# First weights and first memory features in four interleaved pieces, five identity products ahead, x behind the first chunk's weights

## The chip, the core and the metric

The kernel runs on one NeuronCore of a Trainium2 chip. TensorE (PE) multiplies, VectorE (DVE) and ScalarE (ACT) do elementwise work, GpSimd (POOL) does a few masks and powers, and SyncE (SP) issues every transfer (DMA) between HBM and the core's memory. The engines run on their own and wait for each other by semaphores; on each of them instructions run in the order in which they were built. The metric is device microseconds of one execution, the median of three runs. Lower is better.

## The reference, cut to what matters

One layer over 256 tokens of x and 256 tokens of a memory, model width 2048, all in float32:

```python
h = rms_norm(x, norm_mix_g)
x = x + hybrid_mixer(h, ...)              # h @ w_in (18464 columns), two recurrent branches, @ w_out
mem_n = rms_norm(mem, norm_mem_g)
k, v = split(mem_n @ w_kv, 2)             # w_kv: 2048 x 4096
x = x + cross_attention(rms_norm(x, norm_x_g), k, v) @ w_xo
x = x + square(relu(rms_norm(x, norm_ffn_g) @ w_ff1)) @ w_ff2
out = rms_norm(x, norm_final_g)
```

The part at stake is the very beginning: `v`, the right half of `mem_n @ w_kv`, is what the kernel computes first, together with turning x into features.

## The kernel before, in words

**Products in three parts.** Each float32 weight tile `raw` is split into a rounded half `whi` (ACT, L108) and a rest `wlo` (DVE, L111); each activation in the same way into the two halves of a tile `q`. A product is then three matmuls: `q` high by `whi` (L151), `q` high by `wlo` (L152), `q` low by `whi` (L153), each 128x512, summed in PSUM.

**Chunks and quarters.** `chunk` makes 512 output columns from 2048 contracted features, in four quarters `q` of 512 features. `fetch` loads one quarter of weights (1 MB, `raw`, three buffers) and splits it in two halves, so a quarter has two `whi` and two `wlo` tiles and 24 matmuls (4 features blocks by 2 token tiles by 3). The first two chunks are `values(0)` and `values(1)`, then `values(2)` and `values(3)` and the `blocks` of `w_in` follow; below they are chunk 0, chunk 1 and so on. Between chunks 2 and 3 stands the first `blocks` call (L193, L194), which needs the features of x.

**Memory's features.** In chunk 0, `load_mem(c)` loads 512 features of `mem` (`xc`, 0.5 MB), transposes them on PE with the identity (8 transposes, L242), and ACT and DVE make the two halves of `q` (L255, L256) with the norm's gain, which `load_gains` has loaded (`grow`) and transposed (L228). For the first quarter, mem and weights are each loaded in two pieces (`pieces`, `rush`), and the features' transposes are held until after the first rounding (`issue_after(rushed[0])`).

**x's features.** `load_rows(c, x, 0)` loads x in four pieces (0.5 MB each); ACT squares and sums them (L271); their rows' scale goes over PE to `rrow` (L283, L284); PE transposes x (L344, 32 transposes), ACT copies each pair of blocks to `xt` (L347, two buffers), a DMA stores it to `xt_d` (L348), DVE and ACT make `xn` and the features `q` of x (L351, L354, L355). A third `xt` has to wait until the store of the first has landed.

**What sets the order.** The tile framework orders instructions by priorities (`high_priority`) and by when it believes operands are ready; the built order on each engine is then fixed. Every DMA goes over SP's queue, and each takes the next of eight completion counters in turn: a transfer is not issued before the eighth transfer ahead of it has landed. `issue_after` pins an instruction behind another one in SP's or PE's order.

**Small work in the same stretch.** Convolution rows (`cw_rows`), `positions`, `inv_freq`, `gdn_norm_g`, `a_log`, `dt_bias` are loaded early for later use; ACT makes eight decay masks `dm_w` (L514, stored to `dm_d`), sines and cosines (L413, L416), each change of function costing an ACT_TABLE_LOAD.

## Time and profile before

| | us |
|---|---|
| median of three runs | 2099.76 |
| lowest and highest run | 2099.24, 2100.12 |
| profiled execution | 2099.76 |
| its span, from the first to the last instruction | 2098.0 |
| PE busy in it | 2081.5 |
| DVE busy | 1407.9 |
| ACT busy | 1090.9 |

The profiled execution is the median of the runs, so a difference worked out from its trace is also one against the median; 1.76 us of its time lie outside the span. A row of the timeline says when a group of equal instructions began, how long it lasted, engine, line, operation, and in brackets how long the engine had stood idle before it and what ended that. Overlapping matmuls are pipelined, so the distance of starts, not the duration, is the price of one.

### The profile page before, as it was taken

What the parts mean: (1) busy time and instruction counts of PE and PEld (TensorE: products, weight loads), DVE (VectorE), ACT (ScalarE), POOL (GpSimd) and SP (SyncE); (2) the same over time, 40 slices, a digit from 0 to 9 for tenths busy, and PEclk for the clock granted to TensorE, in tenths of its full rate; (3) what the DMA queues carried; (4) which work ended last, traced back from release to release, by engine and by line L of the source; (5) the groups of instructions that cost most, each with busy time, mean ns of one, the idle gap of its engine ahead of it and who ended that gap; (6) DMA issues with size and microseconds to landing.
All of it is one profiled execution on the core that took longest, in us unless ns stands there. A gap on an engine that the chain in (4) does not pass through costs nothing.

```text
span 2098.0 us, 28725 instructions
## 1 busy us (share of the span) xinstructions
PE 2081.5 (99%) x11172; PEld 1797.4 (86%) x11172; DVE 1407.9 (67%) x2217; ACT 1090.9 (52%) x1700; POOL 28.7 (1%) x39
## 2 busy tenths in 40 slices
PE   8999999999999999999999999999999999999998
PEld 6888888888888888888888899888888888888887
DVE  5766788778758885878557666766556555645655
ACT  7674664565446444655456555554434434444444
POOL 0000000000000000000000000000000000000000
PEclk9999999999999999999999999999999999999999
DMA  8787655556555655555458665566566556656653
GB/s 297 242 272 250 198 188 189 164 172 194 180 162 183 193 179 157 188 186 189 160 177 257 193 187 156 177 199 194 188 200 185 198 189 192 192 190 199 185 198 141
DMA packets 314169, 405.91 MB, mean 193 GB/s; under 512 B 16288, under 2 KB 222128, under 8 KB 313904
## 3 DMA queue, kind: packets, MB, share of 16 engines
q1 hardware_dynamic: 313744, 403.55, 60.7%
q8 instruction: 87, 1.43, 0.3%
q10 hardware_dynamic: 288, 0.52, 0.1%
q14 instruction: 50, 0.41, 0.1%
HBM read 390.40 MB, written 13.65 MB: 193 GB/s over the span
## 4 chain that ended last, share of the span: by engine, by line
PE 95%; DMA 2%; ACT 1%; SPq 1%; DVE 1%; issue 0%; POOLq 0%; POOL 0%; ACTq 0%
PE s L193 33%; PE s L194 17%; PE s L152 13%; PE s L153 13%; PE s L151 13%; PE b L689 2%; DMA xt_d<-xt 1%; DMA xc<-x 1%; PE b L595 1%; ACT whi L108 1%; PE b L121 0%; PE b L123 0%; PE b L122 0%; SPq L292 0%; DVE wlo L111 0%
## 5 line engine op out<-in xcount | busy, mean ns | idle before, releaser
L111 DVE TENSOR_TENSOR wlo<-raw,whi 128x1024 fp32r<-128x1024 f32 x702 | 858.1, 1223 | 525.4 <-ACT whi L108 519.0
L108 ACT ACTIVATE whi<-raw 128x1024 fp32r<-128x1024 f32 x702 | 742.8, 1059 | 739.2 <-PE s L153 388.0
L193 PE MATMUL s<-q,whi 128*128 128x512 f32 x3088 | 1062.8, 390 | 0.3 <-DVE q L959 0.3
L194 PE MATMUL s<-q,wlo 128*128 128x256 f32 x3088 | 845.2, 281 | 0.8 <-DVE wlo L111 0.8
L193 PEld LDWEIGHTS s<-q,whi 128*128 128x128 f32 x3088 | 570.9, 188 | 110.0 <-DVE q L959 0.5
L194 PEld LDWEIGHTS s<-q,wlo 128*128 128x128 f32 x3088 | 579.3, 188 | 14.0 <-DVE wlo L111 2.4
L152 PE MATMUL s<-wlo,q 128*128 128x512 f32 x1264 | 495.3, 392 | 1.4 <-DVE wlo L111 1.3
L153 PE MATMUL s<-whi,q 128*128 128x512 f32 x1264 | 493.0, 390 | 0.0
L151 PE MATMUL s<-whi,q 128*128 128x512 f32 x1264 | 453.3, 391 | 1.5 <-ACT q L255 1.5
L152 PEld LDWEIGHTS s<-wlo,q 128*128 128x128 f32 x1264 | 237.6, 188 | 50.9 <-DVE wlo L111 3.4
L151 PEld LDWEIGHTS s<-whi,q 128*128 128x128 f32 x1264 | 237.2, 188 | 50.6 <-ACT q L255 1.9
L153 PEld LDWEIGHTS s<-whi,q 128*128 128x128 f32 x1264 | 237.7, 188 | 48.1
L200 ACT ACTIVATE bo<-s 128x256 f32<-128x256 f32 x193 | 73.1, 379 | 120.3 <-PE s L194 107.3
L201 DVE TENSOR_TENSOR bo<-bo,s 128x256 f32<-128x256 f32 x193 | 80.3, 416 | 46.4 <-ACT bo L200 46.1
L548 DVE SCALAR_TENSOR_TENSOR acc<-bo,cw,acc 128x255 f32<-128x255 f32 (+2 forms) x144 | 66.8, 479 | 1.5
L650 DVE TENSOR_TENSOR pr<-lw,tw 32x31 f32<-32x31 f32 (+15 forms) x124 | 40.4, 326 | 8.8 <-DMA lw<-scr_l 6.9
L652 DVE TENSOR_TENSOR tw<-tw,pr 32x31 f32<-32x31 f32 (+15 forms) x124 | 40.6, 327 | 2.1
L796 ACT ACTIVATE gth<-s 128x512 f32<-128x512 f32 x32 | 18.9, 592 | 23.8 <-PE s L153 18.3
L998 DVE SCALAR_TENSOR_TENSOR res<-s,rstd3q,res 128x512 f32<-128x512 f32 (+1 forms) x32 | 22.3, 735 | 11.7 <-PE s L153 11.7
L987 DVE SCALAR_TENSOR_TENSOR hs<-bo 128x256 f32<-128x256 f32 x64 | 26.9, 421 | 1.1
L990 DVE TENSOR_TENSOR q<-hs,q 128x256 fp32r<-128x256 f32 x64 | 26.9, 420 | 0.8 <-ACT q L989 0.8
L545 ACT ACTIVATE acc<-bo,cw 128x256 f32<-128x256 f32 x48 | 24.1, 503 | 4.5 <-DVE bo L201 4.4
(292 smaller groups left out, 1083.6 us busy)
## 6 DMA issues: line engine op xcount, KB each, us to landing
raw<-w_in SPq DMA_DIRECT2D x144, 1024.0 KB, 5.2
raw<-w_ff SPq DMA_DIRECT2D x128, 1024.0 KB, 5.4
raw<-w_xkv SPq DMA_DIRECT2D x31, 1024.0 KB, 9.2
raw<-w_out SPq DMA_DIRECT2D x16, 1024.0 KB, 6.1
raw<-w_xq SPq DMA_DIRECT2D x16, 1024.0 KB, 6.6
raw<-w_xo SPq DMA_DIRECT2D x16, 1024.0 KB, 5.2
dec_d<-dec_w SPq DMA_DIRECT2D x8, 384.0 KB, 4.6
dec<-dec_d SPq DMA_DIRECT2D x8, 384.0 KB, 3.2
```

The source lines that it names most:

```text
L108: rounding = act.activation(hi, src, AF.Copy)
L111: vec.tensor_sub(lo, src, hi.bitcast(F32))
L151: pe.matmul(o, xh, wh, start=first, stop=False)
L152: pe.matmul(o, xh, wl, start=False, stop=False)
L153: pe.matmul(o, xl, wh, start=False, stop=last)
L193: pe.matmul(ps[b], lh, xhl, start=kk == 0, stop=False)
L194: pe.matmul(ps[b][:, :S], ll, xh, start=False, stop=kk == KT - 1)
L200: act.activation(o, ps[b][:, S:], AF.Copy)
L201: vec.tensor_add(o, o, ps[b][:, :S])
L548: vec.scalar_tensor_tensor(acc[:, d:], ps[:, :S - d], cw[:, j, blk:blk + 1], acc[:, d:], op0=ALU.mult, op1=ALU.add)
L652: vec.tensor_sub(tw[:, j + 1:32, 0:j + 1], tw[:, j + 1:32, 0:j + 1], pv)
L689: pe.matmul(pv[:, i, :], lhs(i), rhs[:, i, :], start=True, stop=True)
```

## The change

Five parts. (1) The first quarter of chunk 0 is loaded in four pieces of 128 features, each a piece of mem (0.125 MB) followed by a piece of weights (0.25 MB); `rush_mem` is called around each weight load. The weights are split piece by piece (128x512 instead of 128x1024), and each piece of features is transposed (2 transposes) and made into `q` on its own. (2) The gains are loaded behind the first pair of pieces instead of ahead of everything. (3) Five products of the identity with itself run ahead on PE. (4) The loads of x may not be issued before the last weights of chunk 0 are. (5) A later chunk (the last `sig_gate` chunk of the mixer) that shared the switch `rush` loads its first weights in one transfer again instead of two; its call of `take_back(0)`, which does nothing, is left out.

```diff
-    rushed = []
-
-    steps = []
+    fetched, steps = [], []
...
-    def fetch(pieces, k, n, rush=False, hold=None, at=(0, 0)):
+    def fetch(pieces, k, n, rush=None, hold=None, at=(0, 0)):
...
-                for ks in ((slice(0, k // 2), slice(k // 2, k)) if rush else (slice(0, k),)):
-                    nc.sync.dma_start(rv[:, ks, off:off + ap.shape[1]], src[:, ks, :])
+                for ks in ([slice(i, i + 1) for i in range(k)] if rush else [slice(0, k)]):
+                    if rush:
+                        rush(0, ks.start)
+                    fetched.append(nc.sync.dma_start(rv[:, ks, off:off + ap.shape[1]], src[:, ks, :]).ins)
+                    if rush:
+                        rush(1, ks.start)
...
-                rounding = act.activation(hi, src, AF.Copy)
-                if rush and not i:
-                    rushed.append(rounding.ins)
-                vec.tensor_sub(lo, src, hi.bitcast(F32))
+                for ks in ([slice(j * n, (j + 1) * n) for j in range(k // 2)] if rush else [slice(None)]):
+                    act.activation(hi[:, ks], src[:, ks], AF.Copy)
+                    vec.tensor_sub(lo[:, ks], src[:, ks], hi[:, ks].bitcast(F32))
...
     with tc.high_priority(offset=200000):
-        load_gains(0, (norm_mem_g,))
+        heat = bank()
+        for i in range(5):
+            pe.matmul(heat[:, :P], ident, ident, start=True, stop=True)
...
     def load_mem(c):
-        with tc.high_priority(offset=50000):
-            xc = load_rows(c, mem, 50000 if c else 100000, 1 if c else 2)
-            with tc.high_priority(offset=100000), nullcontext() if c else tc.issue_after(rushed[0]):
-                ins = to_feature(lambda t, f: xc[:, t, f * P:(f + 1) * P], G_MEM + 4 * c, memq[c])
+        xc = new_rows()
+        with tc.high_priority(offset=100000):
+            load_rows(c, mem, xc)
+        with tc.high_priority(offset=150000):
+            ins = to_feature(lambda t, f: xc[:, t, f * P:(f + 1) * P], G_MEM + 4 * c, memq[c])
         mem_rows.append((xc, ins))
+
+    def rush_mem(now, f):
+
+        if not f and not now:
+            mem_rows.append((new_rows(), None))
+        xc = mem_rows[0][0]
+        if not now:
+            load_rows(0, mem, xc, slice(f * P, (f + 1) * P))
+            return
+        if not f:
+            load_gains(0, (norm_mem_g,))
+        ps = bank()
+        for t in range(NT):
+            pe.transpose(ps[:, t * P:(t + 1) * P], xc[:, t, f * P:(f + 1) * P], ident)
+        qh, ql = (a[:, f, :] for a in memq[0])
+        g = gains[:, G_MEM + f:G_MEM + f + 1]
+        ins = act.activation(qh, ps[:, :S], AF.Copy, scale=g).ins
+        vec.scalar_tensor_tensor(ql, ps[:, :S], g, qh.bitcast(F32), op0=ALU.mult, op1=ALU.subtract)
+        mem_rows[0] = (xc, ins)
...
     values(0)
+    first_weights = list(fetched)
...
-    xcs = [load_rows(c, x, 0) for c in range(4)]
+    xcs = [new_rows() for _ in range(4)]
+    with tc.issue_after(first_weights[-1]):
+        for c in range(4):
+            load_rows(c, x, xcs[c])
```

On PE at the program's start, before (`xc_117` and `xc_162` are the first and second 512 features of mem, `whi_109` and `wlo_110` the first half of the first weights):

```order
L228 MATMUL b_86<-ident_75,grow_84 128x16
L242 MATMUL b_120<-ident_75,xc_117 128x128
L242 MATMUL b_129<-ident_75,xc_117 128x128
L242 MATMUL b_120<-ident_75,xc_117 128x128 x3
L242 MATMUL b_129<-ident_75,xc_117 128x128 x3
L151 MATMUL s0_104<-whi_109,q_98 128x512
L151 MATMUL s1_105<-whi_109,q_98 128x512
L152 MATMUL s0_104<-wlo_110,q_98 128x512
L152 MATMUL s1_105<-wlo_110,q_98 128x512
L153 MATMUL s0_104<-whi_109,q_98 128x512
L153 MATMUL s1_105<-whi_109,q_98 128x512
L242 MATMUL b_164<-ident_75,xc_162 128x128 x4
```

The same place in the changed program (`xc_108` is the first mem tile, `whi_142` and `wlo_143` the first weights; lines have moved by two):

```order
L234 MATMUL b_84<-ident_75 128x128 x5
L228 MATMUL b_113<-ident_75,grow_111 128x16
L326 MATMUL b_116<-ident_75,xc_108 128x128 x2
L326 MATMUL b_123<-ident_75,xc_108 128x128 x2
L326 MATMUL b_130<-ident_75,xc_108 128x128 x2
L153 MATMUL s0_105<-whi_142,q_99 128x512
L154 MATMUL s0_105<-wlo_143,q_99 128x512
L153 MATMUL s1_106<-whi_142,q_99 128x512
L154 MATMUL s1_106<-wlo_143,q_99 128x512
L326 MATMUL b_137<-ident_75,xc_108 128x128 x2
L155 MATMUL s0_105<-whi_142,q_99 128x512
L155 MATMUL s1_106<-whi_142,q_99 128x512
```

The first products stand behind three pieces of mem instead of all four pieces' worth; further down, not shown, the 8 transposes of the third 512 features moved from inside the second quarter to just ahead of it.

On SP, between the loads of x and the first weights of chunk 1 (`raw_502`), before, with the completion counter that each transfer waits for (`raw_290` holds the last weights of chunk 0):

```order
L362 DMA cw_rows_641<-conv_w 48x128 [waits DMAHW0_49]
L362 DMA cw_rows_641<-conv_w 48x128 [waits DMAHW1_49]
L383 DMA posi_667<-positions 128x256 [waits DMAHW2_49]
L98 DMA raw_290<-w_xkv 128x4x512 [waits DMAHW3_49,DVE_49]
L387 DMA invf_669<-inv_freq 64x1 [waits DMAHW4_49]
L387 DMA invf_669<-inv_freq 64x1 [waits DMAHW5_49]
L428 DMA gdng_705<-gdn_norm_g 128x128 [waits DMAHW6_49]
L433 DMA alog_707<-gdn_a_log 16x1 [waits DMAHW7_49]
L434 DMA dtb_708<-gdn_dt_bias 16x1 [waits DMAHW0_49]
L515 DMA dm_d_718<-dm_w_1261 128x256 [waits DMAHW1_49]
L515 DMA dm_d_718<-dm_w_1376 128x256 [waits DMAHW2_49]
L98 DMA raw_502<-w_xkv 128x4x512 [waits DMAHW3_49,DVE_49]
```

The same in the changed program (`xc_377` to `xc_379` are the second to fourth pieces of x, `raw_518` the first weights of chunk 1; the last weights of chunk 0 stand two rows above):

```order
L294 DMA xc_377<-x 128x2x512 [waits DMAHW2_49]
L294 DMA xc_378<-x 128x2x512 [waits DMAHW3_49]
L294 DMA xc_379<-x 128x2x512 [waits DMAHW4_49]
L387 DMA cw_rows_657<-conv_w 48x128 [waits DMAHW5_49]
L387 DMA cw_rows_657<-conv_w 48x128 [waits DMAHW6_49]
L408 DMA posi_683<-positions 128x256 [waits DMAHW7_49]
L412 DMA invf_685<-inv_freq 64x1 [waits DMAHW0_49]
L412 DMA invf_685<-inv_freq 64x1 [waits DMAHW1_49]
L453 DMA gdng_721<-gdn_norm_g 128x128 [waits DMAHW2_49]
L458 DMA alog_723<-gdn_a_log 16x1 [waits DMAHW3_49]
L459 DMA dtb_724<-gdn_dt_bias 16x1 [waits DMAHW4_49]
L99 DMA raw_518<-w_xkv 128x4x512 [waits DMAHW5_49,DVE_49]
```

Chunk 0's last weights now stand ahead of x; chunk 1's first weights stand behind all of x and behind the small loads, two of which (`alog`, `dtb`) wait for the counters of the third and fourth piece of x.

On ACT, around the last copies `xt` of x's blocks, before (`whi_826`, `whi_830` are the last quarter's weights of chunk 2):

```order
L347 ACTIVATE xt_465<-b_460 128x512
L347 ACTIVATE xt_478<-b_473 128x512
L108 ACTIVATE whi_792<-raw_790 128x1024
L354 ACTIVATE q_357<-xn_466 128x2x256
L354 ACTIVATE q_358<-xn_479 128x2x256
L108 ACTIVATE whi_796<-raw_790 128x1024
L347 ACTIVATE xt_491<-b_486 128x512
L108 ACTIVATE whi_826<-raw_824 128x1024
L354 ACTIVATE q_358<-xn_492 128x2x256
L108 ACTIVATE whi_830<-raw_824 128x1024
```

The same in the changed program (`whi_842` and `whi_846` are the last quarter's weights of chunk 2):

```order
L372 ACTIVATE xt_481<-b_476 128x512
L379 ACTIVATE q_373<-xn_469 128x2x256
L372 ACTIVATE xt_494<-b_489 128x512
L112 ACTIVATE whi_842<-raw_840 128x1024
L379 ACTIVATE q_373<-xn_482 128x2x256
L372 ACTIVATE xt_507<-b_502 128x512
L379 ACTIVATE q_374<-xn_495 128x2x256
L112 ACTIVATE whi_846<-raw_840 128x1024
```

The last copy stood ahead of the first half of that quarter's weights and now stands between the two halves. PE's order is the same in both programs from the first `blocks` call on.

## Rows read from the trace of the kernel before

**Rows 1.** The page: span, PE's busy time, and the group of all weight rests
```profile
span 2098.0 us, 28725 instructions
...
PE 2081.5 (99%) x11172; PEld 1797.4 (86%) x11172; DVE 1407.9 (67%) x2217; ACT 1090.9 (52%) x1700; POOL 28.7 (1%) x39
...
L111 DVE TENSOR_TENSOR wlo<-raw,whi 128x1024 fp32r<-128x1024 f32 x702 | 858.1, 1223 | 525.4 <-ACT whi L108 519.0
```

**Rows 2.** Windows (stretch, length, busy by engine, PEclk, DMA share, GB/s)
```profile
86.72:2085.00 1998.28, 1997.25 (x10770) 1728.73 (x10769) 1346.23 (x2097) 1023.35 (x1582) 24.66 (x26) 1.00 0.60 190
...
16.00:18.00 2.00, 2.00 (x10) 1.63 (x9) 2.00 (x4) 1.95 (x6) 0.00 (x0) 1.00 1.05 388
...
75.00:76.00 1.00, 0.73 (x4) 0.42 (x3) 1.00 (x2) 1.00 (x2) 0.00 (x0) 1.00 1.02 289
```

**Rows 3.** Span and mean granted clock of the core
```profile
core 0: 2098.0 us, clock 0.999
```

**Rows 4.** PE's timeline (start, us, engine, line, operation, idle before and releaser)
```profile
5.89 1.54 PE L242 MATMUL b<-ident,xc 128*128 128x128 f32 x6 [0.74 <-DMA xc<-mem]
8.95 1.22 PE L151 MATMUL s<-whi,q 128*128 128x512 f32 x2 [1.52 <-ACT q L255]
9.97 1.10 PE L152 MATMUL s<-wlo,q 128*128 128x512 f32 x2
10.87 1.05 PE L153 MATMUL s<-whi,q 128*128 128x512 f32 x2
...
13.28 0.56 PE L151 MATMUL s<-whi,q 128*128 128x512 f32 x1
...
17.58 0.62 PE L151 MATMUL s<-whi,q 128*128 128x512 f32 x2
18.03 1.03 PE L242 MATMUL b<-ident,xc 128*128 128x128 f32 x8
...
31.44 0.50 PE L152 MATMUL s<-wlo,q 128*128 128x512 f32 x1 [0.57 <-DVE wlo L111]
...
36.56 0.62 PE L151 MATMUL s<-whi,q 128*128 128x512 f32 x2
37.02 0.40 PE L152 MATMUL s<-wlo,q 128*128 128x512 f32 x1
...
51.77 0.50 PE L152 MATMUL s<-wlo,q 128*128 128x512 f32 x1 [0.50 <-DVE wlo L111]
...
75.75 0.50 PE L152 MATMUL s<-wlo,q 128*128 128x512 f32 x1 [0.27 <-DVE wlo L111]
...
81.57 0.50 PE L152 MATMUL s<-wlo,q 128*128 128x512 f32 x1
...
86.72 0.39 PE L193 MATMUL s<-q,whi 128*128 128x512 f32 x1
```

**Rows 5.** ACT's timeline: roundings that waited for a transfer, one table load
```profile
7.48 1.06 ACT L108 ACTIVATE whi<-raw 128x1024 fp32r<-128x1024 f32 x1 [4.12 <-DMA raw<-w_xkv]
...
13.52 1.06 ACT L108 ACTIVATE whi<-raw 128x1024 fp32r<-128x1024 f32 x1 [0.24 <-DMA raw<-w_xkv]
...
34.52 2.01 ACT L108 ACTIVATE whi<-raw 128x1024 fp32r<-128x1024 f32 x2 [3.51 <-DMA raw<-w_xkv]
...
47.08 1.28 ACT L514 ACT_TABLE_LOAD   x1
```

**Rows 6.** SP's timeline: the first issue, and the first weights of chunk 1
```profile
0.79 0.40 SPq L226 DMA_DIRECT2D grow<-norm_mem_g  x1
...
28.84 1.00 SPq L98 DMA_DIRECT2D raw<-w_xkv  x2
```

**Rows 7.** The tile xt (min/median/max ns, first and last start in us)
```profile
L347 ACT ACTIVATE xt<-b x8: 587/598/601, 58.3 to 78.7; 128x512 f32<-128x512 f32 x8
```

**Rows 8.** The chain of waits: stores of xt that ended last
```profile
58.92 4.25 DMA xt_d<-xt
...
72.31 6.32 DMA xt_d<-xt
```

More of the change, by code (lines that the diff above doesn't have):

```diff
@@ L1 @@
 import math
[L2 removed]
+from contextlib import ExitStack
 import numpy as np
@@ L135, in quad_a, with chunk @@
         return new_quad(hqp, 5)
-    def chunk(quads, pieces_of, evac, before=None, hold=None):
+    def chunk(quads, pieces_of, evac, before=None, rush=None, hold=None):
         ps = stream_ps()
@@ L158, in chunk @@
                     before(q)
-                halves = fetch(pieces_of(q), 4, 512, rush=before is not None and q == 0)
-                if before and not q:
-                    before(q)
+                halves = fetch(pieces_of(q), 4, 512, rush=None if q else rush)
                 for i in range(4):
@@ L285, in scale_row, with new_rows, load_rows @@
         return row
-    def load_rows(c, src, rush, pieces=1):
-        xc = kv.tile([P, NT, 512], F32, name="xc", tag="xc", bufs=8)
+    def new_rows():
+        return kv.tile([P, NT, 512], F32, name="xc", tag="xc", bufs=8)
+    def load_rows(c, src, xc, fs=slice(0, 512)):
         rows = src[0, :, c * 512:(c + 1) * 512].rearrange("(t p) d -> p t d", p=P)
-        with tc.high_priority(offset=rush):
-            for ts in (slice(i * NT // pieces, (i + 1) * NT // pieces) for i in range(pieces)):
-                nc.sync.dma_start(xc[:, ts, :], rows[:, ts, :])
-        return xc
+        nc.sync.dma_start(xc[:, :, fs], rows[:, :, fs])
     def row_squares(xc, ssq, c):
```

3 lines of the change are left out of this document (1 added, 2 removed).

## The prediction

> **What bounds the kernel now.** I read the page first: PE is busy for 2081.5 of 2098.0 us [rows 1]. The windows tell where the rest can be: from the first `blocks` call at 86.72 us to 2085 us PE is busy for 1997.25 of 1998.28 us, 1.03 us idle in all [rows 2], and PE's order there is the same in both programs. So the change can only shift the moment at which that stretch begins, and everything behind follows by the same amount. I therefore read PE's timeline up to 86.72 [rows 4] and look for time that isn't matmul work at full pace.
>
> There are three kinds. First, PE's products begin at 8.95, after waiting for `q`, which waited for mem and for the rounding of weights that landed at 7.48 [rows 4, 5]. Second, they begin slowly: two products that wait for nothing start 0.45 us each (9.97 to 10.87), while two later ones take 0.23 each (36.56 to 37.02) [rows 4]. The granted clock of the core is 0.999 over the span [rows 3], which leaves about 2 us of full-rate time, or 4 us at half rate; the pace places them between 8.95 and 13.28: that is 1.2 GHz against 2.4. PEclk in the windows reads 1.00 [rows 2] and is too coarse to show it. Third, three stalls of 0.57, 0.50 and 0.27 us on `wlo` [rows 4].
>
> **The change part by part.** I follow PE through both orders and note how far the changed program is ahead at fixed places.
>
> *First products.* Before, 1,032 KB (8 of gains, 512 of mem, 512 of weights) were on the core at 7.48 [rows 5]. Now the first product needs two weight pieces and three mem pieces, 904 KB: 128 KB less, 0.34 us at 388 GB/s [rows 2], and the bulk starts first, 0.40 us of issue for the gains earlier [rows 6]. That is about 6.75; then the two transposes of the third piece at the slow pace and the copy to `q` behind the second rounding, 0.7 to 0.9 us. First product at about 7.5, 1.4 us earlier; bounds 7.0 and 8.9 (below).
>
> *Small pieces.* A row of mem is now 512 bytes long per piece. The nearest row in the trace is the load of `w_in` in 512-byte rows around 75 us: 289 GB/s with the engines full, against 388 elsewhere [rows 2]. On the 0.5 MB of mem it costs 0.5 us at most; I take half, as half of the bytes in flight are weights. If all 1.5 MB moved at 289 instead of 388 it would be 1.4 us, and the first product would not come earlier at all. In sentences of its own: the Trainium skill, "DMA: Bandwidth & Descriptors", "Rules for kernel authors", asks for transfers of at least 1 MiB for full bandwidth, which speaks against pieces of 0.125 and 0.25 MB; the 289 row agrees in kind, and the slow end above is what the rule would give here.
>
> *Second quarter.* 24 products of the first quarter, the last 2 transposes of the first features, 8 of the second and 8 of the third stand ahead of it now. If the slow pace lasts as long after the first product as before (4.3 us), 9 products and 2 transposes fit until 11.8, the other 15 take 3.4 us, and two groups of 8 transposes some 0.9 us each (18.03 and its row [rows 4]): second quarter at 17.1. If the clock were high from the first product on, the weights decide: 3,080 KB stand up to the second quarter's weights in both programs, and those landed at 13.52 [rows 5]; two roundings of 1.06 and one copy make it 16.0. Before, the second quarter began at 17.58 with 8 transposes still to come, so 18.5 on the same count. Ahead: 1.4 us, 2.5 with the high clock. The five identity products cost nothing, as they stand in a time in which PE has no data; PE then idles again until the pieces land, so I take the slow pace.
>
> *The 0.57 stall.* It fell on the last quarter of chunk 0, whose weights stood behind x. They now stand ahead of x, 6,152 KB into the stream, that is at about 21.6 by 388 GB/s from 13.52, and are wanted at about 29 (31.44 less what is gained). The stall goes: 2.0 us ahead, chunk 0 done at 34.6 instead of 36.56.
>
> *What is late next.* Chunk 1's first weights. On SP they stand behind x, two `cw_rows`, `posi`, `invf`, `gdng`, `alog` and `dtb`; `alog` and `dtb` wait for the third and fourth piece of x. The stream up to the end of x is 8,248 KB, 5.29 MB beyond the 13.52 mark, 13.6 us: 27.2, and I take 27.5, some tenths for the small loads between. Then one issue for `dtb` and one for `raw_518`, at about 28.0; before it was 28.84 [rows 6]. From there to the rounding took 5.7 us [rows 5], so `whi` at 33.7, 1.06 and 1.22 [rows 1, 5] for the two halves: the first product with `wlo` at 36.0 against 37.02 [rows 4]. PE, ready at 35.0, waits 1.0 us. **Ahead: 1.0 us.** This is the step that takes half of the gain. Bounds: 0.7 us to each side, since 6.32 us [rows 8] is what another transfer with 1 MB ahead of it took; 0.3 to 1.7 us ahead.
>
> *Chunk 1 on ACT.* The 0.50 stall at 51.77 came of ACT's queue and goes, as the squares of x now stand behind the rounding concerned: 1.5 ahead. But two more table loads of 1.28 us [rows 5] stand in the queue now, ACT was late there already, as the stall shows, and its roundings for the last quarter come out about 0.25 us late: 1.25 ahead.
>
> *x's copies.* rrow now stands behind chunk 2's first half quarter, so the first `xt` starts at about 63 instead of 58.3 [rows 7]. From `xt` to the next on the same buffer a store has to land: 4.25 us when nothing is ahead of it, 6.32 with a load of 1 MB ahead [rows 8]. Two chains of four copies run side by side; one store of each now has a 1 MB load ahead. That puts the seventh copy at 77.2 and the eighth at 80, where before the eighth was at 78.7 [rows 7]. Behind the seventh stands the rounding of the last quarter's first half (`wlo` at 79.9 to 80.3, PE wants it at 79.8 to 80.0), behind the eighth and one more copy that of its second half (83.3, wanted 82.9). Before, this place was at 81.57 [rows 4] with the weights just in time. So up to 0.27 us of the old stall at 75.75 goes and 0.5 to 0.7 comes: **0.9 us ahead** at the first `blocks` call.
>
> *Costing nothing.* The later chunk with one load instead of two, and the rounding in 512s (four small instructions for two large on ACT and DVE, before PE has work): PE is busy in the one place, and the transfer sets the time in the other.
>
> Sum: 1.4 + 0.6 (stall) - 1.0 (wait for chunk 1's weights) + 0.5 - 0.25 + 0.27 - 0.6 = 0.9 us. 2099.76 - 0.9 = 2098.9 us.
>
> **Rivals.** *A, more of it stays:* chunk 1's weights come 1 us earlier than I count, or the clock is up early, and x's chain stays hidden. Then it is 1.4 to 2.5 at the front plus 0.57, 0.50 and 0.27: 2.7 to 3.8 us, about 2096.5. For it speaks that x's queue is reckoned only to 0.5 us; against it that both waits must be gone. In a sentence of its own: the Trainium skill, "TensorE: Matmul & The Clock Gate", "What's actually happening", says that "the default state is throttled, and activity releases the throttle", by which the five products would start to raise the clock; the slow pace after 1.54 us of transposes from 5.89 on [rows 4] shows that a little activity and a gap are not enough here.
>
> *B, slower:* x's chain. If the copies keep the pace they had, 20.4 us from first to last [rows 7], the eighth is at 83.4 instead of 80; two more ACT instructions and `wlo` put the product that wants it at 86.7, where it stood at about 84.3 (12 products of 0.23 behind 81.57): 0.5 to 2.5 us behind, about 2101.3. It decides from an eighth copy later than 81.5. For it: the 6.32 row, and that 1 MB loads stand between the stores in both orders. Against: the long store of before was the last, where now it is an earlier one.
>
> *C, it does not do what it says:* small pieces at 289 GB/s and a clock that rises as late as before. First product at 8.9; then only the 0.57 stall goes, and the wait for chunk 1's weights takes its place. Within 0.3 of 2099.8.
>
> **How the numbers follow.** Forecast 0.50 (2098.0 to 2099.5), A 0.22 (2096.0 to 2098.0), B 0.18 (2100.0 to 2102.3), C 0.10 (2099.5 to 2100.1). The range takes in C and most of A and B: 2096.2 to 2101.8. A measurement of this kernel can tell about 0.2%, 4.2 us, from no change. All that can be gained before 86.72 is the 3.8 us of A unless the front gives more than the weights' landing allows, so faster gets 0.06; slower needs nearly twice B's price, 0.06; the rest, 0.88, is the same.
>
> **What would show it.** First product near 7.5 and second quarter near 17; no stall in the last quarter of chunk 0; a new wait of about 1 us of PE for `wlo` at the start of chunk 1; two more table loads before 55 us; the eighth `xt` near 80 and waits of some tenths there; first `blocks` product near 85.8. Wrong would be: no wait at chunk 1 (A), or an eighth copy later than 81.5 (B), or a first product at 8.9 (C).

## The result, and the profile after

The changed kernel takes 2102.31 us (median of 21 runs, 2101.46 to 2104.03), the kernel before on the same chip 2099.36 (21 runs): a ratio of 1.0014, interval 1.0008 to 1.0020. That is 2.95 us, or 0.14%, slower: inside the 0.2% that the prediction called the same, but 3.4 us above its 2098.9, half a microsecond outside its range, and on the other side of the kernel before. The profiled execution took 2103.33 us, 1.02 above its median. Of the four cases rival B is the nearest: 2102.31 stands at the upper end of its 2100.0 to 2102.3, and its mark, an eighth copy later than 81.5 us, was passed at 81.77. Its cause came only in part, as shown below.

The page of the changed kernel (span, PE's busy time) against [rows 1]:

```profile
span 2101.6 us, 28758 instructions
...
PE 2085.3 (99%) x11182; PEld 1798.8 (86%) x11182; DVE 1407.9 (67%) x2219; ACT 1092.8 (52%) x1704; POOL 29.9 (1%) x39
```

PE's timeline at the places that [rows 4] shows of before. Columns are start, length, engine, line, operation, and in brackets the idle time before it and what ended it:

```profile
7.89 0.66 PE L326 MATMUL b<-ident,xc 128*128 128x128 f32 x2 [1.80 <-DMA xc<-mem]
8.41 0.79 PE L153 MATMUL s<-whi,q 128*128 128x512 f32 x1
...
18.07 0.48 PE L153 MATMUL s<-whi,q 128*128 128x512 f32 x1
...
36.63 0.73 PE L153 MATMUL s<-whi,q 128*128 128x512 f32 x2 [0.61 <-ACT whi L112]
37.89 0.50 PE L154 MATMUL s<-wlo,q 128*128 128x512 f32 x1 [0.53 <-DVE wlo L113]
...
55.33 0.50 PE L154 MATMUL s<-wlo,q 128*128 128x512 f32 x1 [0.40 <-DVE wlo L113]
...
73.33 0.52 PE L369 MATMUL b<-ident,xc 128*128 128x128 f32 x3 [0.70 <-DVE xn L376]
...
83.16 0.50 PE L154 MATMUL s<-wlo,q 128*128 128x512 f32 x1 [0.51 <-DVE wlo L113]
...
88.28 0.39 PE L193 MATMUL s<-q,whi 128*128 128x512 f32 x1
```

The stall at 31.44 is gone, as forecast, and so are those of 0.50 and 0.27 us. In their place stand five waits, 2.75 us together by the brackets, and the first `blocks` product, at 86.72 before, comes at 88.28: 1.56 us behind, where 0.9 ahead was forecast. A bracket is less than the price of a wait: the two products from 36.63 to 37.89 took 1.26 us, and before the same two took 0.46 (36.56 to 37.02 [rows 4]), so the bracket of 0.53 stands for 0.80.

ACT's timeline at the first two and at the eighth copy of x:

```profile
64.63 1.08 ACT L372 ACTIVATE xt<-b 128x512 f32<-128x512 f32 x2
...
81.77 0.58 ACT L372 ACTIVATE xt<-b 128x512 f32<-128x512 f32 x1
```

SP's queue ahead of chunk 1's first weights (`raw` at 29.96; before it was 28.84 [rows 6]), and the windows (stretch, length, busy by engine, PEclk, DMA share, GB/s) of three stretches:

```profile
12.75 7.11 SPq L294 DMA_DIRECT2D xc<-x  x4
20.84 0.80 SPq L387 DMA_DIRECT2D cw_rows<-conv_w  x2
21.68 0.42 SPq L408 DMA_DIRECT2D posi<-positions  x1
23.69 1.82 SPq L412 DMA_DIRECT2D invf<-inv_freq  x2
26.38 0.36 SPq L453 DMA_DIRECT2D gdng<-gdn_norm_g  x1
28.14 0.33 SPq L458 DMA_DIRECT2D alog<-gdn_a_log  x1
29.53 0.33 SPq L459 DMA_DIRECT2D dtb<-gdn_dt_bias  x1
29.96 0.39 SPq L99 DMA_DIRECT2D raw<-w_xkv  x1
```

```profile
6.00:9.00 3.00, 1.20 (x4) 0.79 (x4) 0.97 (x2) 1.63 (x5) 0.00 (x0) 1.00 0.89 279
16.00:18.00 2.00, 2.00 (x14) 1.69 (x13) 1.62 (x2) 2.00 (x5) 0.00 (x0) 1.00 1.05 388
29.00:31.00 2.00, 2.00 (x10) 1.65 (x10) 1.75 (x5) 0.87 (x4) 0.10 (x1) 1.00 0.06 12
```

The small pieces move at 279 GB/s, the rest of the stream at 388. At 29 to 31 us it has run dry (12 GB/s): eight small transfers stand between x and the next weights, and `alog` and `dtb` are issued only when the third and fourth piece of x have landed.

The chain of waits of the changed kernel, followed back from the last instruction (start, length, what), in the stretch up to the first `blocks` call:

```profile
2.73 4.62 DMA raw<-w_xkv
7.36 12.12 DMA raw<-w_xkv
19.49 10.02 DMA xc<-x
29.53 0.33 SPq L459
29.96 5.48 DMA raw<-w_xkv
35.52 1.07 ACT whi L112
36.61 1.24 DVE wlo L113
37.89 0.50 PE s L154
...
46.60 1.28 ACT L441
47.90 0.42 ACT cos L441
...
50.69 1.26 issue
51.95 0.51 ACT dm_w L539
...
54.05 1.24 DVE wlo L113
55.33 0.50 PE s L154
...
65.25 6.32 DMA xt_d<-xt
71.67 0.61 ACT xt L372
72.30 4.00 DMA xt_d<-xt
76.40 0.60 ACT xt L372
```

It names three things that aren't PE: the transfers up to 35.5, whose last link hangs on `dtb`; ACT's queue from 46.6 to 53 with two table loads in it (L441, and the 1.26 us of "issue" ahead of `dm_w`, which is the load of its table); and x's copies, each waiting for a store to land (6.32 and 4.00 us).

### The profile page after: what moved, and what is told of

It reads as the page before. It is cut to its first block, busy times and chain, and to the rows that moved or that the text cites. A ratio compares the mean times of both kernels' runs of the same rounds, so it can differ in the third digit from the quotient of the medians.

```text
span 2101.6 us, 28758 instructions
## 1 busy us (share of the span) xinstructions
PE 2085.3 (99%) x11182; PEld 1798.8 (86%) x11182; DVE 1407.9 (67%) x2219; ACT 1092.8 (52%) x1704; POOL 29.9 (1%) x39
## 4 chain that ended last, share of the span: by engine, by line
PE 94%; DMA 3%; ACT 1%; DVE 1%; issue 0%; SPq 0%; POOLq 0%; POOL 0%; ACTq 0%; DVEq 0%
PE s L193 33%; PE s L194 17%; PE s L154 13%; PE s L155 13%; PE s L153 13%; PE b L714 2%; DMA raw<-w_xkv 1%; PE b L620 1%; DMA xt_d<-xt 0%; ACT whi L112 0%; DMA xc<-x 0%; PE b L123 0%; PE b L124 0%; PE b L125 0%; DVE wlo L113 0%
## 5 line engine op out<-in xcount | busy, mean ns | idle before, releaser
L113 DVE TENSOR_TENSOR wlo<-raw,whi 128x1024 fp32r<-128x1024 f32 (+1 forms) x704 | 858.5, 1220 | 528.1 <-ACT whi L112 521.9
L112 ACT ACTIVATE whi<-raw 128x1024 fp32r<-128x1024 f32 (+1 forms) x704 | 743.3, 1057 | 737.3 <-PE s L155 379.4
```

Source lines behind the costliest of these rows:

```text
L112: act.activation(hi[:, ks], src[:, ks], AF.Copy)
L113: vec.tensor_sub(lo[:, ks], src[:, ks], hi[:, ks].bitcast(F32))
```

## Experiments

Each was timed against the kernel before on the same chip; "behind" is against its median there. The changed kernel stands at +2.95 us. A median of 11 runs has an interval of some 1.9 us to each side, so differences below 2 us between two variants lean on the trace as well. The table gives places on PE: the start of the 1st, 25th, 97th and 193rd of the 288 products that stand ahead of the first `blocks` call (the first of chunk 0, of its second quarter, of chunk 1 and of chunk 2), that call itself, the median's distance from before, and how far the profiled execution, whose places these are, lies from its own median. Transposes stand at other places in different orders, so the 25th and the 193rd are compared among alike kernels only; ahead of the 97th and of the call the data's transposes are the same in number in all of them.

```
                                     1st   25th   97th  193rd  blocks  median  profiled
before                              8.95  17.58  36.56  61.39   86.72    0      +0.40
before, profiled again              9.94  18.95  37.06  61.19   85.81    -        -
changed                             8.41  18.07  36.63  60.49   88.28  +2.95    +1.02
changed, profiled again             7.92  17.06  36.96  61.67   88.04    -        -
e1  x not held                      8.31  17.93  36.52  62.67   88.03  +4.15    -1.67
e2  before, x held                  9.93  18.91  38.03  62.94   87.35  +1.50    -0.66
e3  no identity                     5.89  16.80  37.43  62.57   88.73  +2.34    +1.46
e4  two pieces                      8.38  16.87  36.35  62.62   85.61  +1.61    -1.51
e10 two small loads late            8.40  17.96  36.21  59.31   87.02  +1.67     0.00
e12 two tables fewer                8.34  18.15  36.92  60.03   86.19  +0.59    +0.43
e5  ten small loads late            7.98  17.36  35.48  57.66   85.08  -0.35    -0.19
e11 two pieces, ten late            8.94  16.97  35.23  57.41   83.56  -1.86    -0.36
e13 as e11, no identity             8.40  15.67  33.94  56.12   82.26  -2.44    -0.88
g3  as e13, x not held              8.40  15.99  36.24  62.77   88.79  +1.26    +2.46
e8  before, ten late                8.91  17.69  35.84  62.10   87.36  +1.60    -0.38
e7  no identity, ten late           7.05  17.34  34.66  58.37   87.71  +2.53    -0.91
e9  three identity, ten late        5.74  16.29  33.65  58.16   87.76  +2.73    -0.46
g4  as e7, masks behind cosine      5.96  17.07  34.42  56.61   85.05  +2.36    -0.13
```

**First theory: x's place is the loss.** e1 undoes part 4 in the changed kernel, e2 does it alone in the kernel before.

```diff
-    with tc.issue_after(first_weights[-1]):
+    if True:
         for c in range(4):
             load_rows(c, x, xcs[c])
```

> The changed kernel with part 4 alone undone: x is loaded where the order puts it without the pin, two of its pieces ahead of the last weights of chunk 0 and two behind them. My theory: the change gains 0.4 us at the front (second quarter 18.07 against some 18.5) and loses 2 us on the way to the first blocks call because x and the small loads behind it delay chunk 1's first weights and x's copies. Then chunk 1's first weights are issued at 28.8 or sooner, the first copy of x starts near 58 to 60, the first blocks product comes at 86.3 to 86.9 as before, and the time is 2099.0 to 2100.0. Rival, the small pieces are the cause (the weights of the second quarter land at 15.28 instead of 13.52, everything queued behind is late): then undoing part 4 gives nothing back and the time stays at 2101.5 to 2102.5.

Measured: 2103.82 us, ratio 1.0020 (1.0012 to 1.0029). That is above both expectations: undoing part 4 gave nothing back, and chunk 1's first weights were waited for just the same (1.06 and 0.53 us at 36.5 and 37.8).

> The kernel before with part 4 alone added: all of x is loaded behind the last weights of chunk 0; pieces, gains and PE's first instructions as before. Theory (x's place costs the time): the 0.57 us stall of chunk 0 goes, the first copy of x starts some 4 to 6 us later than 58.3, the first blocks product is 1 to 2 us later than 86.72, and the time is 2101.0 to 2103.0. Rival (small pieces are the cause): without them the later x is harmless and only the stall's 0.57 us is gained: 2098.5 to 2099.5.

Measured: 2101.17, ratio 1.0009 (1.0000 to 1.0018). It fits the theory's number but not its place: the first `blocks` product was 0.63 behind, with a first product at 9.93, 1 us late before x matters at all (the kernel before, profiled again, shows 9.94 there too). What part 4 moved is a wait: the stall on chunk 0's last weights went, and chunk 1's first weights were waited for instead (0.85 and 0.53 us at 38.03 and 39.29). As the whole of the loss, x's place fell with e1.

**The identity products and the pieces.** e3 sets the count of products to 0; e4 loads the first quarter in two pieces of 256 features.

```diff
-        for i in range(5):
+        for i in range(0):
...
-                for ks in ([slice(i, i + 1) for i in range(k)] if rush else [slice(0, k)]):
+                for ks in ([slice(i, i + 2) for i in range(0, k, 2)] if rush else [slice(0, k)]):
...
-            load_rows(0, mem, xc, slice(f * P, (f + 1) * P))
+            load_rows(0, mem, xc, slice(f * P, (f + 2) * P))
```

> The changed kernel without the five products of the identity; the order then also puts the first products behind two pieces of mem instead of three. Theory: the products between 1.5 and 4.0 us with a gap behind them raise nothing, so the pace of the products turns from 0.43 to 0.23 us a product at the same place, some 4 to 5 us after the first product, and the first product comes about 0.5 us earlier since it no longer waits for the third piece of mem (8.41 there): the time is within 0.5 us of the changed kernel, 2101.5 to 2102.5. Rival (the five products pay): the slow pace lasts 1 us or more longer than in the changed kernel and the time is 2103 or more.

Measured: 2102.01, ratio 1.0013 (1.0004 to 1.0022): the forecast time by another road. The first product came 2.5 us earlier, not 0.5, since the built order now starts on two pieces of mem. At chunk 1 all of it was lost, and more:

```profile
5.89 1.22 PE L153 MATMUL s<-whi,q 128*128 128x512 f32 x2
...
37.43 1.22 PE L153 MATMUL s<-whi,q 128*128 128x512 f32 x2 [3.14 <-ACT whi L112]
```

```profile
9.00:36.00 27.00, 23.92 (x117) 19.18 (x115) 18.95 (x37) 18.32 (x40) 0.70 (x1) 1.00 0.89 313
36.30:43.00 6.70, 5.53 (x12) 3.98 (x13) 4.48 (x7) 5.74 (x7) 0.00 (x0) 0.50 1.06 377
```

The third number from the end is the granted clock: it fell within the wait of 3.14 us, and PE ran at 0.50 (1.2 GHz) for the whole stretch up to 43.0. The first quarter of chunk 1 took 8.40 us, in e5 at full clock 5.44.

> The changed kernel with the first quarter in two pieces of 256 features of mem and of weights each, instead of four of 128; the rest of the change stands, except that the order puts the small loads (convolution rows, positions, frequencies, norm) ahead of chunk 0's last weights. Theory (x's place behind chunk 0's weights is the main loss, the small pieces a small one): the weights of the second quarter land at 14 to 14.6 instead of 15.28, the first product comes at 8.4 to 9.0, chunk 1's first weights are issued behind x all the same, and the time is 2100.5 to 2102.0. Rival (the small pieces alone are the cause): 2098.5 to 2099.8.

Measured: 2101.28, ratio 1.0008 (0.9999 to 1.0017); the first `blocks` product at 85.61, 1.11 us ahead of before. The time is in the theory's range, while the place on PE is better than that, because the profiled execution kept its clock and most of the others did not: the core's mean granted clock is 0.998 in six of the eleven runs, which took 2101.28 to 2103.02 us, and 0.999 in the other five, the profiled one among them, with 2099.49 to 2101.01. (The run with 3.4 us at half clock that is shown further below has 0.998, e3's profiled one 0.997.) In the changed kernel the five runs of 21 with 0.998 are no slower than the rest (medians 2102.03 and 2102.36), so the fall of the clock isn't its loss. The second quarter began at 16.87 instead of 18.07, of which some 0.8 us are 8 transposes that stand behind that place in e4; the waits at chunk 1 stayed (1.21 and 0.53). The pieces may cost something, and the wait behind x is another thing.

**The small loads.** e5 pins all ten of them behind chunk 1's second weights, e8 does the same in the kernel before (also behind chunk 1's second weights, as SP's order shows, not its third), e10 pins only `alog` and `dtb`.

```diff
-            nc.sync.dma_start(cw_rows[48 * j:48 * (j + 1), a, :], ...)
+            with tc.issue_after(fetched[8]): nc.sync.dma_start(cw_rows[48 * j:48 * (j + 1), a, :], ...)
...
-    nc.sync.dma_start(alog, ...)
-    nc.sync.dma_start(dtb, ...)
+    with tc.issue_after(fetched[8]): nc.sync.dma_start(alog, ...)
+    with tc.issue_after(fetched[8]): nc.sync.dma_start(dtb, ...)
```

> The changed kernel with the small loads (convolution rows, positions, frequencies, norm, alog, dtb: ten transfers) pinned behind the second quarter's weights of chunk 1; all else stands. Theory: chunk 1's first weights are late in the changed kernel because ten small transfers stand between x and them on SP, each of which waits until the eighth transfer ahead of it has landed, so that the stream runs dry (25 and 0 GB/s at 29 to 31 us) before these weights are issued at 29.96. Then they are issued before 27 us here, the waits of 0.61 and 0.53 us at 36.63 and 37.89 go, the first blocks product comes at 86.5 to 87.2 instead of 88.28 and the time is 2100.3 to 2101.5. Rival: the amount of data ahead of them decides (x's 2 MB), the waits stay and the time is 2101.8 to 2102.8.

Measured: 2099.17, ratio 0.9998 (0.9989 to 1.0007): all of the 2.95 us came back and 0.35 more, where the theory gave half. Chunk 1's first weights were issued at 20.35, PE had no wait there, and (not foreseen) ACT loaded only one table between 26 and 60 us, since the sine's and cosine's data came later and the masks were all done by then.

> The changed kernel with only alog and dtb pinned behind chunk 1's second weights (the order then also puts the norm's load behind chunk 1's first weights, and the second quarter's weights ahead of mem's second features); positions, frequencies and convolution rows stay where they were, and ACT still loads four tables between sines and masks. Theory: the three transfers between x and chunk 1's first weights that wait for x's own landing are what makes the stream run dry; without them chunk 1's first weights are issued near 26 to 27 instead of 29.96, ACT's wait of 4.37 us for them at 35.52 falls to 2 us or less, the waits of PE at 36.6 and 37.9 go, and about half of the 3.1 us that e5_small_late gave back comes: 2100.2 to 2101.4. Rival (the four table loads on ACT, 2.6 us more than in the kernel before, are the larger part): 2101.4 to 2102.4.

Measured: 2101.01, ratio 1.0006 (0.9998 to 1.0015). Chunk 1's first weights were issued at 25.40, the waits at 36.6 and 37.9 went, ACT kept its four table loads, and waits of 0.53, 0.59 and 0.44 us at 56.9, 72.1 and 81.9 stayed. So the transfers' part is about 1.3 us, with the trace agreeing (the `blocks` call is 1.26 us earlier), and the rest of e5's gain has another source.

> The kernel before with the same ten small loads behind the third quarter's weights of chunk 1 and nothing else; x stays ahead of chunk 0's last weights. Theory: in the kernel before nothing waits at chunk 1, so the earlier weights there are worth nothing; the last weights of chunk 0 come a little earlier and the 0.57 us stall at 31.44 shrinks: 2098.8 to 2099.8. Rival: the small loads' place is worth 1 us or more by itself, by ACT's later queue (the stalls of 0.50 and 0.27 us): 2098.2 or less.

Measured: 2101.12, ratio 1.0006 (0.9997 to 1.0015): neither. Late small loads are no gain by themselves; in the kernel before the 0.57 us stall went (chunk 1 began 0.72 earlier), but ACT was late in chunk 1, though it loaded one table there and not two, and waits of 0.42, 0.44 and 0.53 us at 50.9 to 55.2 came.

**The table loads.** e12 changes one thing in the changed kernel: the last four masks, and with them their stores, stand behind the cosine, so two of the four table loads that begin between 40 and 51 us go.

```diff
-    act.activation(cos, av, AF.Sin)
+    cos_ins = act.activation(cos, av, AF.Sin).ins
...
-        act.activation(dm, dist, AF.Exp, bias=lnk, ...)
+        with (tc.issue_after(cos_ins) if h > 3 else ExitStack()): act.activation(dm, dist, AF.Exp, bias=lnk, ...)
```

> The changed kernel with the last four decay masks pinned behind the cosine on ACT, so that two of its four table loads of 1.28 us between 40 and 51 us go; the loads and PE's order stay. Theory: the stall of 0.40 at 55.33 goes and x's copies start some 2 us sooner, the waits at 73.33 and 83.16 shrink; the waits for chunk 1's first weights stay: 2101.0 to 2102.0, 0.5 to 1.2 us below the changed kernel. Rival (table loads carry the loss): 2099.5 to 2100.5.

Measured: 2099.93, ratio 1.0002 (0.9994 to 1.0011), 2.4 us below the changed kernel: the rival's range. The two intervals just overlap, but ten of the eleven runs (2099.11 to 2101.06) lie below all 21 of the changed kernel (2101.46 and up), and the trace agrees. Up to chunk 2 little is gained (0.46 us; the waits for chunk 1's weights are 1.29 and 0.53 here); from the 193rd product to the `blocks` call it takes 26.16 us instead of 27.79, and none of the waits at 55.33, 73.33 and 83.16 is left. ACT's timeline at the third copy of x, the changed kernel's row and then e12's:

```profile
71.67 0.60 ACT L372 ACTIVATE xt<-b 128x512 f32<-128x512 f32 x1 [4.50 <-DMA xt_d<-xt]
```

```profile
67.22 0.60 ACT L372 ACTIVATE xt<-b 128x512 f32<-128x512 f32 x1 [0.51 <-DMA xt_d<-xt]
```

The copies start only 0.45 us sooner (64.18 for 64.63). But with its roundings earlier ACT lets go of the weight buffers earlier, and the two loads of weights ahead of the first store are issued 1.45 and 2.04 us sooner (the second at 59.86 for 61.90). SP's row, changed and then e12:

```profile
58.02 4.26 SPq L99 DMA_DIRECT2D raw<-w_xkv  x2
```

```profile
56.57 3.67 SPq L99 DMA_DIRECT2D raw<-w_xkv  x2
```

The first store, which took from 65.25 to 71.57 in the changed kernel, is landed by 67.22, 4.35 us sooner. This chain is read from one execution of each kernel. The sizes fit: e10 gives 1.3 us back and e12 2.4, 3.6 together, and e5, which has both, 3.3.

**Together.** e11 is e4 with the ten loads late; e13 is e11 without the identity products, in the same order of everything else.

> The kernel of e4_two_pieces with the ten small loads behind chunk 1's second weights as in e5_small_late; PE's order as in e4. Theory: e4 was 1.0 us below the changed kernel though it waited 1.21 and 0.53 us for chunk 1's weights; these waits go here, so it falls by 2 to 3 us to 2098.0 to 2099.4, at or a little below the kernel before. Rival (the wait moves on, as in e7, to the first weights of chunk 2): 2100.5 to 2101.5.

Measured: 2097.48, ratio 0.9989 (0.9980 to 0.9998), lower than either expectation; no wait of PE between the first product and the first `blocks` call.

> The kernel of e11_two_pieces_small_late without the five products of the identity; every other instruction stands in the same order on every engine, so that this pair shows the products alone. Theory: they stand in idle time with a gap behind them and move nothing: within 0.5 us of e11, and the high clock comes at the same distance behind the first product, 3 to 5 us. Rival: they bring the high clock 1 us or more nearer to the first product, and without them the time is 0.5 us or more above e11's.

Measured: 2096.90, ratio 0.9986 (0.9977 to 0.9995). The five products bring nothing: the pair differs by 0.6 us in their disfavour, which the intervals don't separate. It is the best variant, 2.4 us below the kernel before and 5.4 below the changed one. PE's timeline of e13 at the first `blocks` call:

```profile
82.26 0.39 PE L193 MATMUL s<-q,whi 128*128 128x512 f32 x1
```

> The kernel of e13_two_pieces_no_identity with part 4 undone: x is loaded ahead of chunk 0's last weights again. Theory: with the small loads out of the way, x's place is worth the stall on chunk 0's last weights that the kernel before had (0.57 us at 31.44), somewhat more here since PE is earlier: 2097.4 to 2098.6, 0.5 to 1.7 us above e13. Rival (part 4 was a loss all along, x's copies start sooner without it): 2096.5 or less.

Measured: 2100.43, ratio 1.0007 (0.9998 to 1.0015), 3.5 us above e13, more than expected. In its profiled execution, the slowest of its eleven, chunk 0's last weights, which stand behind x, are waited for (0.89 and 0.53 us at 29.9 and 31.1), and five waits of 0.47 to 0.53 us follow in chunks 1 and 2. So with the small loads late part 4 is a gain, and e1 points the same way in the changed kernel; alone in the kernel before (e2) it was none.

**Where an early start is lost.** e7 puts e3 and e5 together; e9 has three identity products, the most that leave e7's order of PE alone; g4 is e7 with the masks behind the cosine as in e12.

> The changed kernel without the five identity products and with the small loads behind chunk 1's second weights (the two edits of e3_no_identity and e5_small_late together). Theory: without the five products the order starts the weights' products behind two pieces of mem, at 5.89 us instead of 8.41; that gain of 2.5 us was lost in e3 to a wait of 3.14 us for chunk 1's first weights and to the half clock that followed from 36.2 to 43.1 us (3.4 us). With the weights issued before 27 us both go: the first blocks product comes at 82 to 84.5 us, the time is 2095.5 to 2098.5, less than the kernel before. Rival: PE, being earlier, then waits for the data of the next quarters just the same (the stream's rate is the bound up to chunk 1), and the time is 2100 to 2102.

> The same as e7_no_identity_small_late, but with three products of the identity ahead; with three the order of PE stays that of none (first products behind two pieces of mem), from four on it is that of the changed kernel (behind three). Theory: the products raise nothing by themselves, their price in the changed kernel is the order alone: within 0.6 us of e7. Rival: they bring the high clock forward, so that the second level is reached 2 us or more before the moment of e7, and the time is 1 us or more below e7's.

> The kernel of e7_no_identity_small_late (four pieces, no identity products, small loads late) with the masks that stood between sine and cosine, and those behind, pinned behind the cosine on ACT: two table loads fewer. Theory: e7 lost its early start to ACT's queue, whose roundings for chunk 2 stood behind three table loads (PE waits of 1.37, 0.52, 1.32 and 0.38 us); without two of them 2 to 3 us come back: 2098.8 to 2100.2. Rival (the weights' landing in chunk 2 decides, not ACT's queue): 2101 to 2102.5.

Measured: 2102.05 (1.0012, 1.0003 to 1.0021), 2102.25 (1.0013, 1.0004 to 1.0022) and 2101.53 (1.0014, 1.0005 to 1.0023). e7's theory failed: chunk 1 began 2 us ahead of before, but chunk 2's first weights were waited for (1.37 and 0.52 us, behind three table loads on ACT), then x's copies (1.32). e9 is e7 again in time; its profile is 1 us ahead up to chunk 1 and at the same place at the `blocks` call. g4 had two table loads in this stretch where e7 has three, not two fewer, had chunk 2 at 56.61 and the first `blocks` product at 85.05, and lost 1.47 of its 1.67 us lead at the very next product, which waited 1.20 us for the `wlo` of `w_in`. A lead is kept only as far as each following stage has its data early.

**The same kernels again.**

> The kernel before, unchanged, profiled again. If the landing of the row loads at 120 us belongs to the program, it comes 4.2 to 4.3 us behind its issue again and ACT's wait there is 1.3 us or less; if it belongs to the execution it may be anything from 4.2 to 5.2. The stalls on wlo at 31, 52 and 76 us come again within 0.1 us; the time is 2098.8 to 2100.5.

> The changed kernel, unchanged, profiled again. If the landing of the row loads belongs to the program, it comes 5.0 to 5.2 us behind its issue again and PE is 0.85 us further behind at 130 us; if to the execution, from 4.2 on. The first product comes at 8.2 to 8.6, chunk 1's first weights are waited for at 36 to 37 us, x's first copy starts at 64 to 65, and the first blocks product comes at 87.8 to 88.6; the time is 2101.5 to 2103.5.

Measured: 2099.78 and 2102.14 us, one run each. The row loads landed 4.39 us after their issue in the kernel before (4.23 the first time) and 5.09 in the changed one (5.17): ACT's rows there, before, before again, changed, changed again:

```profile
124.17 1.07 ACT L509 ACTIVATE dec_w<-row,bcol 128x64 f32<-128x64 f32 x4 [1.28 <-DMA row<-crow]
```

```profile
123.37 1.07 ACT L509 ACTIVATE dec_w<-row,bcol 128x64 f32<-128x64 f32 x4 [1.39 <-DMA row<-crow]
```

```profile
126.58 0.59 ACT L534 ACTIVATE dec_w<-row,bcol 128x64 f32<-128x64 f32 x2 [2.13 <-DMA row<-crow]
```

```profile
126.36 0.83 ACT L534 ACTIVATE dec_w<-row,bcol 128x64 f32<-128x64 f32 x3 [2.14 <-DMA row<-crow]
```

So 0.85 us of the loss at 130 us came in both profiles of the changed kernel and in neither of the kernel before: it belongs to the program, though the ten transfers ahead of these loads are the same. Why they land later isn't settled: e1, e3, e4 and e10, whose order of SP is near the changed kernel's, show 5.0 to 5.2 too, the others 4.0 to 4.8. The front did not repeat so well. The kernel before had none of its three stalls the second time, against the expectation, with a first product 1 us later; its first `blocks` product was 0.91 us earlier, and yet the time was the same. The changed kernel's first product came at 7.92, earlier than expected; it waited 1.58 and 0.53 us at chunk 1, and its clock fell behind that, as e3's did:

```profile
36.96 0.73 PE L153 MATMUL s<-whi,q 128*128 128x512 f32 x2 [1.58 <-ACT whi L112]
38.22 0.69 PE L154 MATMUL s<-wlo,q 128*128 128x512 f32 x1 [0.53 <-DVE wlo L113]
```

```profile
38.40:41.80 3.40, 3.40 (x9) 2.66 (x10) 2.89 (x5) 3.38 (x5) 0.00 (x0) 0.50 1.05 382
```

With PE held up there, nothing was waited for in chunk 2: the eighth copy came at 81.53, much as in the first profile, and the first `blocks` product at 88.04 instead of 88.28. So the waits for x's copies in the first profile and PE's slow stretch in the second seem to be two forms of one loss, set by when x's features are there.

## Why the prediction was wrong, step by step

**First products, +1.4 forecast: about +0.4.** The first product came at 8.41 (7.92 the second time), not 7.5, inside the bounds of 7.0 and 8.9. The term that was mis-sized is the price of the small pieces. The prediction took 0.25 us for them; the stream ran at 279 GB/s between 6 and 9 us, the third piece of mem was waited for until 7.89, and the 3,080 KB up to the second quarter's weights landed at 15.28, not 13.52. That is somewhat more than the 289 GB/s end, 1.4 us, which the text named and gave only to rival C. No run parts the pieces' pace from SP's issues: ten transfers instead of six stand ahead of the second quarter's weights, which are issued at 5.69 instead of 3.66. On the prediction's own count of transposes the second quarter's 18.07 is 0.4 ahead of 18.5. With two pieces instead of four chunk 1's first product came 0.25 us earlier (35.23 in e11, 35.48 in e5); e11's median is 1.5 us below e5's, though the intervals overlap, and most of that arises behind this place. The Trainium skill advises at least 1 MiB per transfer ("DMA: Bandwidth & Descriptors", "Rules for kernel authors"). The trace agrees in kind, with 279 against 388 GB/s. The row of 289 GB/s that the prediction set beside the rule is no sign for it: it shows a load of 1 MB in short rows, together with stores.

**Second quarter's clock.** In the first profile it behaved as assumed: the changed kernel's pace turned from 0.43 to 0.23 us a product near 13.2, as before. In the second it turned at 11.1, 3.2 us behind the first product instead of 4.8. The mean granted clock of 0.999, from which the prediction worked out its 4 us at half rate, does not speak of this place: it comes from the end of the program, where PE has no more work (window of the kernel before, clock third from the end):

```profile
2096.00:2098.00 2.00, 0.00 (x0) 0.00 (x0) 0.00 (x0) 0.00 (x0) 0.00 (x0) 0.50 0.32 115
```

Of the start's clock only the pace tells. The products of the identity are not seen to raise it: in e11, with them, the pace turned 2.7 us behind the first product (8.94 to 11.64), in e13, without them, 1.3 behind (8.40 to 9.70). Both are less than the 3 to 5 expected, and they differ by no more than two profiles of the changed kernel do. What the products do is move the order: with three of them it is still that of none (e9), with five the build puts the first products behind three pieces of mem. "The five identity products cost nothing" was right of their time and blind to that, but the early start that they forgo isn't kept either (e7, g4).

**The 0.57 stall, -0.6: right** that it goes; by distance of starts it was worth a little more (the two products ahead of it took 1.18 us, 30.26 to 31.44, instead of 0.46).

**Chunk 1's weights, -1.0.** The mechanism was right and named `alog` and `dtb`; the wait was 1.14 us by the brackets. But chunk 0 was done at about 35.9, not 34.6, and the weights were issued at 29.96, not 28.0: x landed 2 us later than 388 GB/s from an on-time start would have it, and SP stood behind that landing. The first product with `wlo` came at 37.89, not 36.0, so 1.9 of the 2.5 us by which the first `blocks` product missed its forecast place (88.28 for 85.8) stood there already: 1.3 from chunk 0's late end, 0.6 from the wait. e10 shows the price, about 1.3 us, in the transfers' order alone.

**Two more table loads, -0.25: the step that failed most, some 2.4 us.** They were counted for one rounding that comes out late. ACT's order is one queue: two loads of 1.28 us also delay the squares of x, the roundings behind them, and through these the release of weight buffers and the issue of the weights' loads, behind which the first store of x then queues. e12 gives 2.4 us back for these two loads; its masks and their stores moved with them, and no run parts the two. PE shows the same size: from chunk 1's first `wlo` product to the `blocks` call the changed kernel takes 50.39 us, e12 48.01; the waits behind x's copies are part of that. Against the kernel before, 49.70, it lost only 0.7 us, where 0.1 was forecast, since a second error nearly cancels the first: the old waits in this stretch were worth 1.7 us, not the 0.77 of their brackets (e2 and e4, without any wait there, take 48.06 and 47.99).

**x's copies, -0.6 + 0.27: the chain's length was right, its start was not.** Forecast were copies at 63, 77.2 and 80 (first, seventh, eighth); the changed kernel shows 64.63, 79.36 and 81.77. From first to eighth that is 17.1 us for 17.0, and 1.6 us late from the first copy on: on ACT a rounding of 1.06 us (63.41) stands between chunk 2's first half quarter and the first copy, and 63 leaves no room for it. e12 shows 64.18, 77.03 and 79.44, and that its last copies meet the forecast is luck: a start 1.2 late and a chain of 15.3 us, with a first store that took 2.4 us. "4.25 us when nothing is ahead of it" was misread too: in the kernel before a load of 1 MB was issued at 56.02, 2.9 us ahead of that store. Rival B, given 0.18, expected the old pace of 20.4 us from first to last; its mark was passed by the late start instead, so its time came in part by luck.

**"Everything behind follows by the same amount": wrong.** PE's order is the same behind 86.72, but its data isn't landed at the same distance. The changed kernel was 1.56 us behind at the first `blocks` call, 2.41 behind the row loads at 130 us, and 3.4 at the end; the second time it was 1.33, 2.18 and 2.2. What came in both is the 0.85 us at the row loads; 0.75 us near 374 us came only once. And a lead can shrink: e13's 4.46 us became 3.81 at the `kr` and `vr` loads near 1112 us, and the 0.91 us of the kernel before, profiled again, became nothing. A shift below 1 us at one place, in one execution, is no forecast of the time. The later chunk of part 5 shows no cost, as assumed: in the second profile the distance moves by 0.05 us between 140 us and the end. Parts 2 and 5 were undone in no run by themselves.

**The range.** It ended 0.5 us too low. B's own range, 2100.0 to 2102.3, was cut at 2101.8 by its chance; the knock-on behind the first `blocks` call, excluded by the sentence above, was not in it.

## What to carry to other kernels

Where a queue is served in order, an instruction that is put in it is priced by everything behind it up to the next slack, not by the one consumer that one looks at: two table loads of 1.28 us on an engine busy for half the span cost some 2.4 here. Small loads between large ones are not small when each waits for an earlier transfer to land; put them behind the next large load that something waits for (in the kernel before, where nothing waited for it, that gave nothing: e8). Price a wait by the distance of starts, not by its bracket. And an earlier start is worth only what the later stages can take: look for the next transfer that would be late, for each of them, before counting it.

## What the runs showed of the hardware

A wait of PE costs more than its length when the clock falls after it. With 3.14 us of waiting (e3) the granted clock was 0.50 for the 6.7 us shown; after 1.58 and 0.53 us (the changed kernel again) for 3.4 us; after 0.61 and 0.53 us (its first profile) and after 1.29 and 0.53 us (e12) the products kept their pace. In e4 the runs with a lower mean clock are some 2 us longer (medians 2101.74 and 2099.84). The Trainium skill tells of the clock as throttled unless activity releases it ("TensorE: Matmul & The Clock Gate", "What's actually happening"); the runs add that waits of 1.58 and 0.53 us in the middle of a busy stretch were once enough to lose it. The other surprise is the row load: the same instruction behind the same ten transfers landed after 4.0 to 5.2 us, depending on the program, with a cause that these runs don't show.
